# Hybrid encoder layer on one core: merged last down-projection groups, the v cast on GpSimd, and roots of norms left in PSUM

## The chip, the cores and the metric

The kernel runs on one core of a Trainium2 chip. The metric is the device time of one execution in microseconds; the time of the kernel before is the median of three runs. A profile of one execution on the chip goes with it.

## The reference

One layer of a streaming encoder, for a prompt of 2048 frames and a sample of 32 frames that continues a stream with 2048 cached frames. Everything is fp32, d_model is 1024.

```python
h = x + rmsnorm(mixer(rmsnorm(x, g_mix_pre)), g_mix_post)
y = h + rmsnorm(conv_ffn(rmsnorm(h, g_ffn_pre)), g_ffn_post)

def mixer(h):                     # one projection for both groups
    q, k, v, z, xbc, dt_raw = split(h @ w_in)        # 512 each for q, k, v, z; 768; 8
    attn = stick_breaking(q, k_all, v_all)           # 8 heads x 64, strictly causal
    xh, B, C = split(silu(causal_dwconv(xbc, 4 taps)))
    y = ssd_scan(xh, softplus(dt_raw + dt_bias), -exp(a_log), B, C) + d_skip * xh
    y = rmsnorm(y * silu(z), g_ssm_out)              # the gated norm
    return concat(rmsnorm(attn, g_attn_out), y) @ w_out

def conv_ffn(h):                  # D_FF = 2816
    gate, up = split(h @ w_up)
    return (gelu(causal_dwconv(gate, 3 taps)) * up) @ w_down
```

Results are y, the k and v rows, the SSD states and the convolution tails. `rmsnorm` divides by the root of the mean square plus 1e-6.

## The kernel before

Activations lie with channels on partitions and tokens on columns. The tokens are cut into four blocks (0 to 3) of 512, 512, 512 and 544 columns; the last holds the 32 sample frames. Each matrix product is made of three: weights and activations are split into a high part, rounded to fp32r, and the low rest, and high x high, high x low and low x high are summed in PSUM (`dense`, L123). `weight` (L95) loads a raw weight, casts its high part on ScalarE (L107), subtracts on GpSimd (L108) and keeps the result in device memory under a key; later blocks load the kept parts with one DMA (L103). Weights rotate through two buffers `w` in phase one and three afterwards.

Phase one (`phase_in`) goes block by block: the convolution channels (`wbx`, conv on VectorE at L336 and L340, sigmoid on ScalarE at L344), the v projection with tokens on partitions (two halves of 260 columns for each 128 tokens; ScalarE copies them out of two PSUM buffers at L371 or L373, casts the high part `vs` at L383, GpSimd subtracts at L384, and DMAs store both), the SSD scan, the next block's norm (`prep`, scaling at L262), k and q, the gate (`gate`, L580) and the gated norm (`gate_norm`). The gated norm takes the squares' sum over partitions with a ones-matmul of 512 columns, a ScalarE square root and a VectorE reciprocal (`rstd`, L140 to L146) and scales at L602; ScalarE and GpSimd then split into `khi` and `klo` (L606, L608). The other norms use `rstd_steps`: the sum is taken with tokens on partitions (matmuls of one column, L165), VectorE adds epsilon, GpSimd raises to the power -1/2 (L183), and a matmul with the identity spreads the root over the partitions again (L194). With `stay` the root is read from PSUM, else ScalarE copies it out (L200).

Then attention of the next block and the output and FFN work of the last one (`Tail.stream`) are woven together by `fill`; block 3's tail runs alone from about 2430 us. The FFN goes by units of 128 channels: `up` makes a unit (22 in all), `down` multiplies a group of units (GROUPS: six of three, then two of two) with `w_down` and adds to eight output tiles f0 to f7. In the last block the last two groups run for each half of the columns (272) apart; `finish` then takes the root of that half (with `of`, the epsilon of the earlier norm in it, L178 to L185), scales (L1096), adds the residual and stores.

The order on each engine comes from the tile framework's scheduler, which places instructions by a simulated time line; queues are then served in order. SP issues all DMAs.

## Time and profile before

| | us |
|---|---|
| median of three runs | 2948.01 (2941.73 to 2950.02) |
| the profiled execution, its span | 2949.99, 2948.2 |
| TensorE busy | 2815.8 (96%) |
| VectorE busy | 1712.5 (58%) |
| ScalarE busy | 1261.2 (43%) |
| GpSimd busy | 1261.3 (43%) |

In the rows, PE is TensorE, PEld its weight loads, DVE is VectorE, ACT ScalarE, POOL GpSimd, SP the engine that issues DMAs (SPq its queue). Busy time of TensorE is modelled at its ends. `PEclk` is the clock that TensorE was granted: 1.00 is 2.4 GHz, 0.50 is 1.2. A name such as `w` or `rn_v` is a tile of the program; `a<-b` writes a from b. Behind a row, `[2.54 <-ACT v L373]` says that the engine was idle for 2.54 us before it and what ended that.

### The profile page before, as it was taken

To read this page: it belongs to the slowest core of one execution; us is meant where nothing else is said; L and a number is where in the kernel's file an instruction comes from. 1 tells how busy PE (TensorE), PEld (TensorE's weight loads), DVE (VectorE), ACT (ScalarE), POOL (GpSimd) and SP (SyncE) were. 2 spreads that over 40 slices of the span, in tenths; PEclk is the share of its full clock that TensorE was granted. 3 is DMA by queue.
4 is the path that set the end of the run, shared out by engine and by line. 5 is a ranking of instruction groups with operands and counts; after the bars stand their busy time and mean duration, and the time that the engine had idled before them with its cause. 6 is when DMAs were issued, how large, how long until landed. Compare 5 with 4: busy or idle time off the path is not lost.

```text
span 2948.2 us, 44882 instructions
## 1 busy us (share of the span) xinstructions
PE 2815.8 (96%) x16687; PEld 2425.0 (82%) x16687; DVE 1712.5 (58%) x2668; ACT 1261.2 (43%) x2552; POOL 1261.3 (43%) x1061
## 2 busy tenths in 40 slices
PE   8999999989889999999999999999999999999996
PEld 6777778877778888887788888978888879999996
DVE  7666576557774555537744456786666653533334
ACT  5344444337765444436433334654444433311111
POOL 4555555435766655547322223553323224411113
PEclk9999999989999999999999999999999999999998
DMA  5646454648677777777555556656544455755555
GB/s 179 183 154 175 146 169 128 170 141 266 235 260 250 271 249 276 266 255 243 197 185 182 175 178 221 236 182 215 175 167 166 167 192 180 240 177 174 176 177 174
DMA packets 251308, 586.36 MB, mean 199 GB/s; under 512 B 66155, under 2 KB 107763, under 8 KB 222547
## 3 DMA queue, kind: packets, MB, share of 16 engines
q1 hardware_dynamic: 251090, 583.49, 59.7%
q8 instruction: 133, 2.18, 0.3%
q14 instruction: 85, 0.69, 0.1%
HBM read 445.70 MB, written 137.69 MB: 198 GB/s over the span
## 4 chain that ended last, share of the span: by engine, by line
PE 74%; DVE 14%; DMA 6%; ACT 2%; issue 2%; POOL 1%; SPq 1%; DVEq 0%; POOLq 0%; ACTq 0%
PE o L123 36%; PE u L123 12%; PE t L123 10%; PE z L815 4%; PE pa L856 4%; PE pt L834 3%; PE o L364 2%; DVE xc L340 2%; DMA acB<-acD 1%; DMA w<-wS_out 1%; DVE prow L666 1%; DVE acB L440 1%; DVE x L262 1%; DVE xc L336 1%; DVE xlo L272 1%
## 5 line engine op out<-in xcount | busy, mean ns | idle before, releaser
L123 PE MATMUL o<-xhi,w 128*128 128x512 f32 (+2 forms) x3968 | 1044.4, 345 | 31.9 <-ACT xhi L286 7.9
L123 PEld LDWEIGHTS o<-xhi,w 128*128 128x128 f32 x3968 | 697.3, 192 | 125.4 <-issue 8.1
L123 PE MATMUL o<-xlo,w 128*128 128x512 f32 (+2 forms) x1984 | 683.4, 344 | 6.4 <-DVE xlo L272 3.6
L108 POOL TENSOR_TENSOR w<-wraw,w 128x1024 fp32r<-128x1024 f32 (+2 forms) x156 | 366.8, 2352 | 237.2 <-ACT w L107 212.3
L671 POOL TENSOR_TENSOR beta<-beta,prow 128x512 f32<-128x512 f32 (+3 forms) x256 | 253.8, 993 | 439.6 <-DVE prow L666 354.0
L123 PEld LDWEIGHTS o<-xlo,w 128*128 128x128 f32 x1984 | 380.0, 192 | 51.3 <-DVE xlo L272 5.3
L123 PE MATMUL o<-ah,w 128*128 128x512 f32 x992 | 344.6, 405 | 5.3 <-DVE f L1075 4.6
L123 PE MATMUL u<-xhi,w 128*128 128x512 f32 x1056 | 349.2, 398 | 0.0
L1029 POOL TENSOR_TENSOR y<-y,gb 128x512 f32<-128x512 f32 (+1 forms) x88 | 115.8, 1317 | 534.8 <-ACT gb L1028 534.8
L839 DVE TENSOR_TENSOR wt<-pt,wt 128x512 fp32r<-128x512 f32 (+2 forms) x320 | 191.5, 602 | 153.2 <-ACT wt L838 150.5
L666 DVE TENSOR_TENSOR_SCAN prow<-gam,prow,z 128x513 f32<-128x513 f32 x192 | 245.1, 1277 | 58.9 <-ACT beta L664 56.4
L838 ACT CAST wt<-pt 128x512 fp32r<-128x512 f32 (+2 forms) x320 | 166.9, 526 | 208.6 <-PE pt L834 206.4
L123 PEld LDWEIGHTS u<-xhi,w 128*128 128x128 f32 x1056 | 198.9, 188 | 46.8
L123 PEld LDWEIGHTS o<-ah,w 128*128 128x128 f32 x992 | 188.2, 190 | 47.6 <-DVE f L1075 5.7
L663 ACT ACTIVATE gam<-z 128x512 f32<-128x512 f32 (+2 forms) x320 | 173.0, 541 | 98.8 <-PE z L815 67.4
L123 PE MATMUL u<-xlo,w 128*128 128x512 f32 x528 | 209.3, 396 | 0.0
L1021 DVE SCALAR_TENSOR_TENSOR y<-gb,cv,y 128x512 f32<-128x512 f32 (+1 forms) x176 | 163.2, 928 | 72.9 <-ACT y L1019 69.9
L107 ACT CAST w<-wraw 128x1024 fp32r<-128x1024 f32 (+2 forms) x156 | 155.2, 995 | 99.3 <-PE o L123 80.8
L123 PE MATMUL o<-al,w 128*128 128x512 f32 x496 | 197.7, 399 | 0.0
L834 PE MATMUL pt<-ident,beta 128*128 128x128 f32 x1088 | 181.1, 278 | 9.6 <-DVE rn_v L175 4.4
L123 PE MATMUL t<-xhi,w 128*128 128x272 f32 x960 | 188.9, 292 | 1.0 <-DMA w<-wS_out 0.7
L856 PE MATMUL pa<-wt,v 128*64 128x256 f32 (+3 forms) x1152 | 174.7, 281 | 8.6 <-ACT wt L838 5.4
(272 smaller groups left out, 5102.3 us busy)
## 6 DMA issues: line engine op xcount, KB each, us to landing
w<-wS_up SPq DMA_DIRECT2D x132, 1024.0 KB, 4.8
w<-wS_dn SPq DMA_DIRECT2D x72, 768.0 KB, 4.8
wS_up<-w SPq DMA_DIRECT2D x44, 1024.0 KB, 4.8
w<-wS_out SPq DMA_DIRECT2D x39, 1024.0 KB, 7.1
wraw<-wup SPq DMA_DIRECT2D x44, 512.0 KB, 5.8
k<-kS SPq DMA_DIRECT2D x80, 256.0 KB, 4.3
v<-vS SPq DMA_DIRECT2D x80, 256.0 KB, 4.2
wS_dn<-w SPq DMA_DIRECT2D x24, 768.0 KB, 4.4
```

What stands on the lines that cost most here:

```text
L107: nc.scalar.copy(hi[:, :n, :], raw[:, :n, :])
L108: nc.gpsimd.tensor_tensor(lo[:, :n, :], raw[:, :n, :], hi[:, :n, :].bitcast(F32), op=ALU.subtract)
L123: mm = nc.tensor.matmul(ps[:, : c1 - c0], l[:, k, :], at(r, k0 + k)[:, c0:c1], start=first and i == 0 and k == 0, stop=last and i == 2 and ...
L663: nc.scalar.activation(g[:, c0:512], z, AF.Sigmoid, scale=-0.125)
L666: nc.vector.tensor_tensor_scan(back(pr), back(g), z[:, 0:1].to_broadcast([P, n + 1]), self.kn.ones[:, 0:1] if prev is None else prev, op0= ...
L671: eng.tensor_tensor(b[:, :n], b[:, :n], pr[:, c0 + 1 : 513], op=ALU.mult)
L815: mm = nc.tensor.matmul(z[:, :n], q[:, P * b : P * b + P], k[:, :n], start=e == 0, stop=e == 1 and kc < s)
L834: mm = nc.tensor.transpose(t[:, P * j : P * j + P], w[:, P * j : P * j + P], kn.ident[:])
L838: nc.scalar.copy(hi, t)
L839: nc.vector.tensor_tensor(lo, t, hi.bitcast(F32), op=ALU.subtract)
L856: nc.tensor.matmul(av[:m, 2 * P * p + c0 : 2 * P * p + 2 * P], v[:, j, :m], wt[:, rest, j, c0:], start=kc == s and p + j + rest == 0, stop ...
L1021: nc.vector.scalar_tensor_tensor(y[:, :W], gb[:, i : i + W], kn.col(wc + i), y[:, :W], op0=ALU.mult, op1=ALU.add)
```

## The change

Four edits. First, in the last block the groups (18, 2) and (20, 2) become one group (18, 4): `down` is called once for each half, with weights of both kept groups loaded into one buffer by two DMAs. Second, the cast of v's high part goes from ScalarE to GpSimd. Third, the root of `prep` stays in PSUM for blocks of 512 columns, and the gated norm of blocks 0 to 2 takes its root by `rstd_narrow`, with `stay`; `rstd` is gone. Fourth, the FFN's post-norm root: GpSimd now multiplies the earlier norm's value by epsilon, once, and keeps it as `rcol`, and `finish` adds it in one VectorE step where it had four around the power.

```diff
@@ weight @@
-        if key in self.kept:
-            nc.sync.dma_start(w[:, :, :n, :].bitcast(F32), self.kept[key][:])
+        keys = key if isinstance(key, list) else [key]
+        if keys[0] in self.kept:
+            m = n // len(keys)
+            for i, k in enumerate(keys):
+                nc.sync.dma_start(w[:, :, m * i : m * i + m, :].bitcast(F32), self.kept[k][:])
             return hi, lo
@@ rstd: removed; rstd_steps @@
-        v = pool.tile([P, 8], F32, name="rn_v") if rcol is None else rcol
+        v = pool.tile([P, 8], F32, name="rn_v")
...
+                nc.vector.scalar_tensor_tensor(
+                    v[rows, cols], ps[rows, cols], 1.0 / width, of[rows, cols], op0=ALU.mult, op1=ALU.add
                 )
-            nc.vector.tensor_tensor(v[:, :nb], v[:, :nb], of[:, :nb], op=ALU.mult)
-            nc.vector.tensor_scalar(v[:, :nb], v[:, :nb], EPS, 0.0, op0=ALU.add, op1=ALU.add)
-        nc.gpsimd.tensor_tensor(v[:, :nb], v[:, :nb], self.mhalf[:, :nb], op=ALU.pow)
-        if of is not None:
-            nc.vector.tensor_tensor(v[:, :nb], v[:, :nb], of[:, :nb], op=ALU.mult)
+        w = v
+        if rcol is not None:
+            w = pool.tile([P, 8], F32, name="rn_w")
+        nc.gpsimd.tensor_tensor(w[:, :nb], v[:, :nb], self.mhalf[:, :nb], op=ALU.pow)
+        if rcol is not None:
+            nc.gpsimd.tensor_scalar(rcol[:, :nb], v[:, :nb], EPS, 0.0, op0=ALU.mult, op1=ALU.add)
+        v = w
@@ phase_in @@
-        r = kn.rstd_narrow(rp, psm, "st", [sq], nt, D)
+        r = kn.rstd_narrow(rp, psm, "st", [sq], nt, D, stay=nt <= 512)
...
-            nc.scalar.copy(vs[:, 0, :], v[:, :512])
+            nc.gpsimd.tensor_copy(vs[:, 0, :], v[:, :512])
...
-        for _ in gate_norm(kn, s, xc, tm, lambda *r: kn.rstd(rp, psm, *r, tag="rstd2")):
+        for _ in gate_norm(kn, s, xc, tm, lambda sq, *r: kn.rstd_narrow(rp, psm, "st", [sq], *r, stay=True)):
@@ Tail @@
     GROUPS = [(3 * i, 3) for i in range(6)] + [(18, 2), (20, 2)]
+    LAST = GROUPS[:6] + [(18, 4)]
...
-        j0, n = self.GROUPS[g]
+        j0, n = (self.LAST if s == NSB - 1 else self.GROUPS)[g]
...
-                kn.wp, kn.a["wdn"][c // 2][:, 2 * j0 : 2 * j0 + 2 * n, :], 2 * n, key=("dn", g, c)
+                kn.wp, kn.a["wdn"][c // 2][:, 2 * j0 : 2 * j0 + 2 * n, :], 2 * n, key=[("dn", 6, c), ("dn", 7, c)] if n == 4 else ("dn", g, c)
...
-                if j == j0 and g and g < len(groups) - 1:
+                if j == j0 and g and (g < len(groups) - 1 or s == NSB - 1):
...
-                for e in range(2):
+                for e in range(1 if s == NSB - 1 else 0, 2):
                     yield from self.down(s, g - 1 + e, acts[g - 1 + e], t, e == 1)
```

The scheduler's order moves with it. Three places follow, with the number of a row in its engine's order at its start; the number behind a name tells the buffers apart.

At the end of the program, on SP, before: `w` are the weight buffers, `wS_dn_6_0` the kept weights of group 6 for output tiles 0 and 1, `o_fconv` a result that is read from unit 21's buffer `gb`.

```order
1266 L103 DMA w_28349<-wS_dn_6_0_12138 128x2x512
1267 L103 DMA w_28367<-wS_dn_6_2_12161 128x2x512
1268 L1015 DMA o_fconv<-gb_28224 128x2
1269 L1016 DMA o_fconv<-gb_28224 128x2
1270 L103 DMA w_28385<-wS_dn_6_4_13285 128x2x512
1271 L103 DMA w_28403<-wS_dn_6_6_13308 128x2x512
1272 L103 DMA w_28422<-wS_dn_7_0_13359 128x2x512
1273 L103 DMA w_28444<-wS_dn_7_2_13390 128x2x512
```

The same place now:

```order
1271 L106 DMA w_28376<-wS_dn_6_0_12164 128x2x512
1272 L106 DMA w_28376<-wS_dn_7_0_13391 128x2x512
1273 L106 DMA w_28411<-wS_dn_6_2_12187 128x2x512
1274 L106 DMA w_28411<-wS_dn_7_2_13422 128x2x512
1275 L1008 DMA o_fconv<-gb_28250 128x2
1276 L1009 DMA o_fconv<-gb_28250 128x2
1277 L106 DMA w_28448<-wS_dn_6_4_13317 128x2x512
1278 L106 DMA w_28448<-wS_dn_7_4_13481 128x2x512
```

Each buffer is filled by two DMAs, and the two stores of `gb` stand behind four loads, not two. On VectorE, in the second half of the same place, before (`t` is an output tile in PSUM, `f_24951` to `f_24958` are the tiles f0 to f7; the scalings at L1096 and additions at L1100 belong to the first half):

```order
2180 L1096 SCALAR_TENSOR_TENSOR f_24958<-f_24958,cv,rstd 128x272
2181 L1075 TENSOR_TENSOR f_24951<-t,f_24951 128x272
2182 L1100 TENSOR_TENSOR f_24952<-f_24952,xr 128x272
2183 L1075 TENSOR_TENSOR f_24952<-t,f_24952 128x272
2184 L1075 TENSOR_TENSOR f_24953<-t,f_24953 128x272
2185 L1100 TENSOR_TENSOR f_24954<-f_24954,xr 128x272
```

And now (`f_24977` to `f_24984` are f0 to f7):

```order
2138 L1068 TENSOR_TENSOR f_24981<-t,f_24981 128x272
2139 L161 MEMSET rn_v 128x8
2140 L1089 SCALAR_TENSOR_TENSOR f_24977<-f_24977,cv,rstd 128x272
...
2147 L1089 SCALAR_TENSOR_TENSOR f_24984<-f_24984,cv,rstd 128x272
2148 L1068 TENSOR_TENSOR f_24982<-t,f_24982 128x272
2149 L1093 TENSOR_TENSOR f_24978<-f_24978,xr 128x272
2150 L1093 TENSOR_TENSOR f_24980<-f_24980,xr 128x272
2151 L1068 TENSOR_TENSOR f_24983<-t,f_24983 128x272
```

The eight scalings stood ahead of the second half's first output tile and now stand behind its fifth. In the v stretch of block 1, on ScalarE, before (`v<-o` is a copy of half a v tile, `t<-xc` a sigmoid behind the convolution):

```order
141 L373 COPY v_1883<-o_1833 128x260
142 L373 COPY v_1883<-o_1834 128x260
143 L383 CAST vs_1888<-v_1883 128x512
144 L344 ACT_TABLE_LOAD
145 L344 ACTIVATE t_1638<-xc_1601 128x512
146 L344 ACTIVATE t_1676<-xc_1601 128x512
147 L373 COPY v_1943<-o_1893 128x260
148 L373 COPY v_1943<-o_1894 128x260
```

And now:

```order
134 L365 COPY v_1889<-o_1839 128x260
135 L365 COPY v_1889<-o_1840 128x260
136 L365 COPY v_1949<-o_1899 128x260
137 L365 COPY v_1949<-o_1900 128x260
138 L365 COPY v_2009<-o_1959 128x260
139 L336 ACTIVATE t_1644<-xc_1607 128x512
140 L336 ACTIVATE t_1682<-xc_1607 128x512
141 L365 COPY v_2009<-o_1960 128x260
```

Five copies stand ahead of the first sigmoid where two did, and the cast and a table load are gone. At the end of block 0, on GpSimd, before (`w<-wraw` is a weight's low part, `klo` the low part of the gated norm's output):

```order
60 L108 TENSOR_TENSOR w_1717<-wraw_1718,w_1717 128x1024
61 L108 TENSOR_TENSOR w_1755<-wraw_1756,w_1755 128x1024
62 L608 TENSOR_TENSOR klo_1543<-xc_236,khi_1541 128x512
63 L608 TENSOR_TENSOR klo_1550<-xc_236,khi_1548 128x512
64 L108 TENSOR_TENSOR w_1793<-wraw_1794,w_1793 128x1024
65 L608 TENSOR_TENSOR klo_1557<-xc_236,khi_1555 128x512
66 L608 TENSOR_TENSOR klo_1564<-xc_236,khi_1562 128x512
```

And now (`rn_v` is the gated norm's root):

```order
64 L111 TENSOR_TENSOR w_1723<-wraw_1724,w_1723 128x1024
65 L174 TENSOR_TENSOR rn_v_1538<-rn_v_1538,mhalf_76 128x4
66 L111 TENSOR_TENSOR w_1761<-wraw_1762,w_1761 128x1024
67 L111 TENSOR_TENSOR w_1799<-wraw_1800,w_1799 128x1024
68 L600 TENSOR_TENSOR klo_1549<-xc_236,khi_1547 128x512
69 L600 TENSOR_TENSOR klo_1556<-xc_236,khi_1554 128x512
70 L111 TENSOR_TENSOR w_2408<-wraw_2409,w_2408 128x1024
71 L600 TENSOR_TENSOR klo_1563<-xc_236,khi_1561 128x512
```

The root's power stands between weights, and the low parts come behind one weight more (`w_1799` is the weight that was `w_1793`).

## Rows read from the trace of the kernel before

**Rows 1.** The page: busy us, share of span, instructions; TensorE.

```profile
PE 2815.8 (96%) x16687; PEld 2425.0 (82%) x16687; DVE 1712.5 (58%) x2668; ACT 1261.2 (43%) x2552; POOL 1261.3 (43%) x1061
```

**Rows 2.** Stretches: length, busy by engine (instructions), granted clock, DMA share, GB/s.

```profile
0.00:640.00 640.00, 588.70 (x3479) 493.71 (x3480) 424.16 (x710) 277.81 (x442) 323.79 (x198) 0.97 0.53 159
...
2892.00:2949.00 57.00, 32.26 (x220) 30.06 (x218) 29.70 (x71) 8.80 (x20) 23.19 (x26) 0.82 0.62 188
```

**Rows 3.** TensorE's waits: waiter, releaser; us in total, times, longest.

```profile
PE o L364 <- ACT v L373: 7.5, 3, 2.9
PE u L194 <- DVE rn_v L185: 6.3, 3, 3.5
...
PE t L123 <- DMA w<-wS_dn: 5.7, 7, 1.2
```

**Rows 4.** The chain that ended last: start, us, what; in the last block.

```profile
2868.30 6.03 PE t L123 x48
```

**Rows 5.** TensorE's time line in the tail: start, us, instruction [idle before].

```profile
2896.46 0.36 PE L123 MATMUL t<-ah,w 128*128 128x272 f32 x1 [1.05 <-DMA w<-wS_dn]
...
2924.25 0.39 PE L123 MATMUL t<-ah,w 128*128 128x272 f32 x1 [2.05 <-DVE f L1075]
```

**Rows 6.** Time line of all engines from 2930 us to the end.

```profile
2930.00 0.44 DVE L1075 TENSOR_TENSOR f<-t,f 128x272 f32<-128x272 f32 x1 [0.31 <-PE t L123]
...
2932.30 1.16 PE L165 MATMUL u<-ones,fsq 128*128 128x1 f32 x6 [2.34 <-POOL fsq L776]
...
2934.25 0.86 POOL L183 TENSOR_TENSOR rn_v<-rn_v,mhalf 128x3 f32<-128x3 f32 x1 [2.00 <-DVE rn_v L182]
...
2935.45 1.43 PE L194 MATMUL u<-ident,rn_v 128*128 128x128 f32 x6 [2.00 <-DVE rn_v L185]
...
2937.34 4.89 DVE L1096 SCALAR_TENSOR_TENSOR f<-f,cv,rstd 128x272 f32<-128x272 f32 x8 [2.03 <-ACT rstd L200]
```

**Rows 7.** DMA issues, 2890 to 2935 us: count, KB each, us to landing.

```profile
w<-wS_dn SPq DMA_DIRECT2D x14, 512.0 KB, 4.7
```

**Rows 8.** Time line of all engines, 2885 to 2900 us: unit 21.

```profile
2890.66 0.66 ACT L1026 ACTIVATE gb<-y 128x546 f32<-128x546 f32 x1 [2.87 <-DMA o_fconv<-gb]
...
2895.96 1.34 POOL L1044 TENSOR_TENSOR al<-y,ah 128x544 fp32r<-128x544 f32 x1 [1.72 <-ACT ah L1043]
```

**Rows 9.** TensorE's time line in phase one, two of its waits.

```profile
220.40 0.39 PE L364 MATMUL o<-wvhi,xhi 128*128 128x260 f32 x1 [2.54 <-ACT v L373]
...
314.89 0.77 PE L123 MATMUL o<-xhi,w 128*128 128x512 f32 x1 [2.86 <-DVE t L580]
```

**Rows 10.** ScalarE's time line in the v stretch of block 1.

```profile
218.79 1.29 ACT L344 ACTIVATE t<-xc 128x512 f32<-128x512 f32 x2 [4.28 <-DVE xc L340]
```

**Rows 11.** The v split by line: ns min/median/max, first and last start, forms.

```profile
L383 ACT CAST vs<-v x16: 602/620/627, 62.1 to 556.4; 128x512 fp32r<-128x512 f32 x16
...
L384 POOL TENSOR_TENSOR vs<-v,vs x16: 1283/1292/3138, 62.8 to 557.1; 128x512 fp32r<-128x512 f32 x16
```

**Rows 12.** Stretches behind those two waits of TensorE; the granted clock is third last.

```profile
221.80:225.20 3.40, 3.40 (x18) 3.40 (x17) 3.40 (x7) 2.07 (x4) 1.20 (x1) 0.50 0.22 66
...
314.00:320.70 6.70, 5.81 (x14) 4.59 (x15) 3.52 (x5) 0.63 (x1) 2.37 (x1) 0.50 0.41 146
```

**Rows 13.** Two scalings by line: root in SBUF (L262), in PSUM (L762).

```profile
L262 DVE SCALAR_TENSOR_TENSOR x<-x,cv,rstd x24: 736/748/2922, 152.7 to 480.6; 128x512 f32<-128x512 f32 x16, 128x544 f32<-128x544 f32 x8
...
L762 DVE SCALAR_TENSOR_TENSOR att<-att,cv,u x32: 467/475/500, 775.0 to 2444.5; 128x256 f32<-128x256 f32 x24, 128x272 f32<-128x272 f32 x8
```

**Rows 14.** VectorE's time line: the scalings of x for blocks 1 and 2.

```profile
152.68 9.70 DVE L262 SCALAR_TENSOR_TENSOR x<-x,cv,rstd 128x512 f32<-128x512 f32 x8
...
306.61 7.53 DVE L262 SCALAR_TENSOR_TENSOR x<-x,cv,rstd 128x512 f32<-128x512 f32 x8 [0.45 <-ACT rstd L200]
```

**Rows 15.** GpSimd's time line there.

```profile
158.85 2.98 POOL L108 TENSOR_TENSOR w<-wraw,w 128x1024 fp32r<-128x1024 f32 x1 [2.49 <-ACT w L107]
```

**Rows 16.** VectorE's time line at the gated norm of block 0.

```profile
189.63 3.35 DVE L146 RECIPROCAL rstd<-rstd 128x512 f32<-128x512 f32 x1 [11.43 <-ACT rstd L143]
```

More of the change, by code (lines that the diff above doesn't have):

```diff
@@ L133, in dense @@
             self.mark(mm)
-    def rstd(self, pool, psp, sq, n, width, tag="rstd", pt="st"):
-        nc = self.nc
-        r = pool.tile([P, 544], F32, name=tag)
-        for c0, c1 in tiles_of(n):
-            ps = psp.tile([P, 512], F32, name=pt)
-            nc.tensor.matmul(
-                ps[:, : c1 - c0], self.ones[:], sq[:, c0:c1], start=True, stop=True
-            )
-            nc.scalar.activation(
-                r[:, c0:c1], ps[:, : c1 - c0], AF.Sqrt, bias=self.eps[:], scale=1.0 / width
-            )
-        nc.vector.reciprocal(r[:, :n], r[:, :n])
-        return r
     def rstd_narrow(self, *args, **kw):
@@ L168, in rstd_steps @@
                 )
-        v = pool.tile([P, 8], F32, name="rn_v") if rcol is None else rcol
+        v = pool.tile([P, 8], F32, name="rn_v")
         if e:
             nc.vector.memset(v[:], 1.0)
-        if of is None:
-            if e:
-                nc.vector.tensor_scalar(v[:e, nf:nb], ps[:e, nf:nb], 1.0 / width, EPS, op0=ALU.mult, op1=ALU.add)
-            nc.vector.tensor_scalar(v[:, :nf], ps[:, :nf], 1.0 / width, EPS, op0=ALU.mult, op1=ALU.add)
-        else:
-            for rows, cols in ((slice(0, P), slice(0, nf)),) + (((slice(0, e), slice(nf, nb)),) if e else ()):
+        for rows, cols in ((slice(0, P), slice(0, nf)),) + (((slice(0, e), slice(nf, nb)),) if e else ()):
+            if of is None:
+                nc.vector.tensor_scalar(
+                    v[rows, cols], ps[rows, cols], 1.0 / width, EPS, op0=ALU.mult, op1=ALU.add
+                )
+            else:
                 nc.vector.scalar_tensor_tensor(
-                    v[rows, cols], ps[rows, cols], 1.0 / width, of[rows, cols], op0=ALU.mult, op1=ALU.mult
+                    v[rows, cols], ps[rows, cols], 1.0 / width, of[rows, cols], op0=ALU.mult, op1=ALU.add
                 )
-            nc.vector.tensor_tensor(v[:, :nb], v[:, :nb], of[:, :nb], op=ALU.mult)
-            nc.vector.tensor_scalar(v[:, :nb], v[:, :nb], EPS, 0.0, op0=ALU.add, op1=ALU.add)
-        nc.gpsimd.tensor_tensor(v[:, :nb], v[:, :nb], self.mhalf[:, :nb], op=ALU.pow)
-        if of is not None:
-            nc.vector.tensor_tensor(v[:, :nb], v[:, :nb], of[:, :nb], op=ALU.mult)
+        w = v
[5 more added lines that the diff above has]
+        v = w
         yield
@@ L1124, in stream @@
             done = (i for h in (0, SBS[s - 1][1] // 2) for i in self.finish(s - 1, h, h + 256, self.f))
-        groups = self.GROUPS
+        groups = self.LAST if s == NSB - 1 else self.GROUPS
         tiles = tiles_of(nt)
```

## The prediction

> **What bounds the kernel now.** I read the page first, then the table of stages, then TensorE's waits, and only then single stretches. TensorE is busy for 2815.8 us of 2948.2 [rows 1], so only idle TensorE time and TensorE time at the lower of its two clock levels can be won. By stage [rows 2], TensorE is idle for 51 us of phase one (0 to 640 us) and for 25 of the 57 from 2892 us on; in the attention and the FFN between them it is 97% full, and the change touches little there. Of the waits [rows 3] three are met by edits: ScalarE's v copies 7.5 us, the last multiply of the finish's root (L185) 6.3, and the last down-projection weights 5.7. The profiled execution took 2949.99 us (span 2948.2 and 1.8 around it); the sum is made against that, and it lies 2.0 above the median of the runs, 2948.01.
>
> **1. Merged last groups: the tail.** Two groups of two units become one of four. In the last block the matmuls stay 192: 48 take 6.03 us [rows 4], so 0.1256 each and 24.1 in all. They begin one load's work (24 matmuls, 3.0 us) before the wait of 1.05 us that ends at 2896.46 [rows 5], at 2892.4, and end at 2930.0, when VectorE starts on the last output tile [rows 6]: 37.6 us. Of the 13.5 lost, at most 2.6 are the small matmuls of the first half's finish (1.16 and 1.43 for such a pair in the end, at the low clock [rows 6]; I take 1.6), the rest are waits: for weights, like that one, and 2.05 at 2924.25 for an output tile that VectorE was late to empty [rows 5]. A 512 KB load lands 4.7 us after its issue [rows 7], is used up in 12 matmuls, 1.5 us, and there are three buffers: 4.7 + 1.5 over 3 is 2.1 us for each 1.5 of work. After, a buffer holds 1 MB for 24 matmuls, 3.0 us; the second 512 KB lands some 1.7 us after the first (an estimate: the three buffers pass one in 2.1 us, and their queue is not full), so 4.7 + 1.7 + 3.0 over 3 is 3.1 against 3.0. The weight waits are nearly gone; I leave 1 us.
>
> A new wait comes in its place. Before, the first eight output tiles used units 18 and 19 alone. Now each needs unit 21, whose low part (al) is written at 2895.96 and takes 1.34 [rows 8]: ready at 2897.3. In SP's queue one more load stands right ahead of the two output DMAs for which ScalarE waited 2.87 us [rows 8]; the whole chain behind (square, VectorE, sigmoid, GpSimd, VectorE, cast) moves by about 0.5, so 2897.8. TensorE can do ten matmuls, 1.3 us, and then stands from 2893.6 to 2897.8. The other 182 end at 2897.8 + 22.9 + 1.6 + 1.0 = 2923.3, not 2930.0: 6.7 us earlier.
>
> VectorE eats a part. In its new order the eight scalings of the first half (4.89 us a set [rows 6]) stand ahead of output tiles 5, 6 and 7 of the second. The scalings can start when the broadcast in tile 5 is copied, at about 2919.2, and end at 2924.1; three additions from PSUM at 0.44 and three others about as long lead to 2926.8 for tile 7, against 2930.4. Squares come 1.5 us apart rather than 0.75 and no longer queue at GpSimd: 3.9 gained at the ones-matmul of 2932.30. Behind it the root has one VectorE step for three before GpSimd's power, and none between the power's end at 2935.11 and the broadcast at 2935.45: 0.7 in all. Sum 4.6. The stand of 4.2 us may cost a stretch of lower clock afterwards (as below, up to 1.7), most of it inside waits that are left. **Taken: -4.0**; bounds 0 (every microsecond of the first wait lost) and -7.5.
>
> **2. The other roots.** L181, L182 and L185 go for six finishes of earlier blocks; the price of each is the same 0.7. TensorE waited there twice more, 6.3 less 2.0 [rows 3, 6] = 4.3 us. **Taken: -1.0**; bounds 0 and -2.2. The extra GpSimd multiply of the FFN roots (eight, at most the 0.86 of the power each [rows 6]) is read only a block later; if GpSimd were late there, its 7 us would show.
>
> **3. Phase one, in four pieces.**
> (a) V stretch of block 1. TensorE waited 2.54 us at 220.40 [rows 9], as the v copy stood in ScalarE's queue behind two sigmoids which waited 4.28 us for VectorE's convolution [rows 10]. The change takes the cast (0.62 [rows 11]) out, and the new order puts five v copies ahead of the first sigmoid. Blocks 0, 2 and 3 keep copies behind sigmoids. After the wait the clock was granted at 0.50 from 221.8 to 225.2 [rows 12], the 1.2 GHz level: 1.7 us of work lost. Of 4.2 in all I take -2.5.
> (b) Roots in PSUM. The scalings of x took 0.75 us in the median, but up to 2.92; the scaling of the attention output, with its root in PSUM, never exceeds 0.50 (475 ns for half the columns) [rows 13]. The eight of block 1 took 9.70 us and those of block 2 7.53 [rows 14]: three long ones, one of which fills the end of a weight's subtraction on GpSimd, 158.85 to 161.83 [rows 15]. The Trainium skill, "SBUF — State Buffer" (Who interferes with whom), says that a VectorE instruction with two SBUF inputs contends with a GpSimd one that reads SBUF, and one with a single SBUF input does not; the two lines agree. Blocks 1 and 2 (not 3, whose root goes to SBUF as before) so win 3 x 2.15 = 6.5 us of VectorE, and the copy of the root on ScalarE goes from each chain. Behind them stand the gate's products: 2.86 us idle at 314.89 [rows 9], then 6.7 us at 0.50 [rows 12]. I take -3.0 of 6.2.
> (c) The gate norm's root. 3.35 us of reciprocal go, but VectorE had been idle for 11.43 us before it [rows 16], so that gains nothing by itself. In TensorE's new order the broadcast stands some 25 matmuls of 512 columns behind the ones-matmul (25 x 0.1256 x 512/272 = 5.9 us), so the root comes no earlier, and at the end of block 0 GpSimd's low parts (klo) come one weight later, 24 matmuls or 5.7 us; the next convolution, whose tile they free, starts up to 5 us later. What covers it is that the SSD of block 1 also waits for the last v copy, at the end of the stretch. +1.5; bounds -2 and +5.
> (d) The cast on GpSimd: the trace has no such cast; ScalarE's 0.62 and GpSimd's two-input subtraction of 1.29 [rows 11] bound it. 16 of them are 10 to 21 us on an engine busy for half of phase one, beside VectorE's convolutions, which have two SBUF inputs. The nearest row is the subtraction, on the same engine, so I count about 1 us each. VectorE loses what a long scaling loses, at most a cast's length, 4 x 1.29 = 5.2 us a stretch; a third of its time is free, so +1.0; bounds 0 and +15 (three stretches, as in the last rival). The Trainium skill, in the section named above, speaks against this edit: whichever of the two engines comes second waits for the whole of the other's instruction.
> **Taken: -3.0**; bounds -11 and +10. The schedule is rebuilt between 600 and 800 us as well (the sample's scores move by some rows); I take 0 there, with 3 either way.
>
> Sum: 2949.99 - 4.0 - 1.0 - 3.0 = **2942 us**, 6 below the median: inside 0.3% (8.8 us, about what a measurement of this kernel can tell from no change; 2939.2 to 2956.8).
>
> **Rivals.**
> *Phase one opens up.* The waits of (a) and (b) go whole with their clock: 4.2 + 6.2 + 1 = 11.4, with the tail at 4.6 and 1 for the roots: 2933. For it: the long scalings end with a GpSimd instruction, and both waits stand right behind VectorE. Against: (c) gives some back.
> *Nothing moves.* The wait for unit 21 eats the weight waits: if the second load of a buffer lands 3 us rather than 1.7 after the first, the six later loads cost some 1 us each, and the low clock after the stand the rest. Roots that come 25 matmuls later are no earlier, so that half of the change does not do what it says. 2947 to 2950, say 2948.
> *Slower: GpSimd holds the convolution.* The casts delay VectorE in the stretches of blocks 0, 2 and 3, where v copies still stand behind sigmoids, by 4 x 1.29 each: 15.5, less 5 of tail and roots: 2960. It decides once the sigmoids come more than a V tile (2.9 us) later than now. For it: TensorE's waits of 2.87 at 381.70 and 2.09 at 542.30 are of this kind already, the rest of the 7.5 [rows 3]. Against: VectorE is idle a third of phase one [rows 2].
>
> **How the numbers follow.** Forecast 0.45 (2938 to 2946), phase one opens 0.25, nothing moves 0.20, slower 0.10. Faster by over 0.3%: nearly all of the second and a quarter of the first, 0.35. Slower: most of the last, 0.10. Within: 0.55. The range is 2931 to 2955: down to the second case with 2 to spare, up to half of the slower one; about 0.15 is left out.
>
> **What would show it.** Tail: one TensorE wait of 4 to 5 us near the end of the up-projection with GpSimd's al as releaser, hardly any for weights afterwards, and tiles 5 to 7 emptied after the eight scalings. Roots: no x scaling over 1 us in blocks 1 and 2. V stretches: block 1 without a wait for v copies, blocks 2 and 3 with one. Wrong: weight waits still of 5 us in the tail, a cast of 2 us, or convolutions that stand behind casts and push v copies in every block.

## The result, and the profile after

The changed kernel is slower. Its median is 2963.28 us (six runs, 2958.18 to 2967.91) against 2947.69 for the kernel before; the ratio is 1.0046, with a 95% interval of 1.0028 to 1.0064. The medians differ by 15.6 us, and the interval stands for 8 to 19 us more, where 6 less were forecast; the time lies outside the stated range. The profiled execution took 2967.91 us, its span is 2966.1, 17.9 more than before. In the changed kernel most line numbers are about eight lower than before (the v cast is L375, its subtraction L376, the convolution L328 and L332, the first product with `da` L400), while `dense` is L126.

Work has not grown. This is the line that answers to [rows 1]:

```profile
PE 2818.6 (95%) x16729; PEld 2430.9 (82%) x16729; DVE 1672.2 (56%) x2628; ACT 1240.0 (42%) x2525; POOL 1283.8 (43%) x1088
```

TensorE is busy 2.8 us longer, VectorE 40 us less, ScalarE 21 less, GpSimd 22 more. So about 15 of the 17.9 us are TensorE's idle time. Where it lies is read from four stretches that begin and end with the same instructions: up to the first score of the attention, from there to a wait of 4.37 us that both kernels have, from there to a matmul of the last up-projection that stands behind a wait in both (2.74 us for `y` on VectorE before, 5.32 for its weight now), and the rest. First the kernel before (columns as in [rows 2]):

```profile
0.00:643.80 643.80, 592.50 (x3509) 497.51 (x3510) 424.16 (x710) 278.20 (x443) 324.33 (x198) 0.97 0.53 159
643.80:771.10 127.30, 112.07 (x814) 87.41 (x813) 94.24 (x155) 91.27 (x220) 68.97 (x69) 0.95 0.77 244
771.10:2559.00 1787.90, 1745.98 (x9510) 1477.04 (x9510) 1053.47 (x1488) 819.54 (x1745) 794.41 (x731) 0.99 0.63 215
2559.00:2948.20 389.20, 365.21 (x2856) 363.02 (x2856) 140.59 (x317) 72.19 (x145) 73.64 (x63) 0.97 0.54 179
```

and the changed kernel:

```profile
0.00:657.40 657.40, 596.31 (x3552) 500.45 (x3552) 404.91 (x709) 257.34 (x416) 341.18 (x210) 0.96 0.53 155
657.40:792.00 134.60, 116.24 (x814) 93.05 (x813) 94.13 (x156) 90.90 (x220) 69.58 (x76) 0.90 0.73 231
792.00:2582.20 1790.20, 1742.08 (x9511) 1474.82 (x9511) 1042.90 (x1473) 820.82 (x1746) 801.19 (x740) 0.99 0.63 214
2582.20:2966.10 383.90, 363.92 (x2856) 362.57 (x2856) 130.29 (x292) 70.97 (x143) 71.88 (x62) 0.97 0.54 181
```

The differences are +13.6, +7.3, +2.3 and -5.3. The tail gained a little more than was forecast for it; phase one and the 130 us behind it lost four times as much. In the second stretch the clock column falls from 0.95 to 0.90 with the same 814 matmuls.

TensorE's waits (as in [rows 3]) name the place. The waits for the v copies of blocks 1 to 3 fell from 7.5 to 5.6 us (that of block 0 grew from 1.5 to 3.3) and the wait for the last down weights is gone from the list, but a wait that before was too short for it now stands at its head:

```profile
PE st L400 <- DVE da L398: 12.6, 2, 9.3
...
PE u L186 <- POOL rn_v L174: 6.7, 3, 4.1
...
PE o L356 <- ACT v L365: 5.6, 3, 2.6
PE u L155 <- POOL fsq L768: 5.5, 1, 5.5
```

`da` is the last of the small softplus steps on VectorE behind the v projection; the SSD scan of a block begins with it. The long wait is that of block 1. GpSimd's time line there, in the changed kernel:

```profile
215.62 5.18 POOL L375 CAST vs<-v 128x512 fp32r<-128x512 f32 x1 [2.04 <-ACT v L365]
220.89 6.38 POOL L376 TENSOR_TENSOR vs<-v,vs 128x512 fp32r<-128x512 f32 x1
230.07 0.91 POOL L375 CAST vs<-v 128x512 fp32r<-128x512 f32 x1 [2.79 <-DMA vS<-vs]
231.06 2.37 POOL L376 TENSOR_TENSOR vs<-v,vs 128x512 fp32r<-128x512 f32 x1
236.26 0.61 POOL L375 CAST vs<-v 128x512 fp32r<-128x512 f32 x1 [2.83 <-DMA vS<-vs]
...
238.23 2.66 POOL L251 TENSOR_TENSOR sq<-sq,t 128x512 f32<-128x512 f32 x2
```

A cast that takes 0.61 us when VectorE is quiet took 5.18, and the subtraction behind it 6.38 where 1.29 is its median [rows 11]. Beside them VectorE ran two unbroken series of convolution steps, each step at its usual 0.74 us, and then, 26 us after the first series began, the eight softplus steps (five of them shown):

```profile
215.62 4.71 DVE L332 SCALAR_TENSOR_TENSOR xc<-raw,cv,xc 128x512 f32<-128x512 f32 x7
...
220.75 5.38 DVE L332 SCALAR_TENSOR_TENSOR xc<-raw,cv,xc 128x512 f32<-128x512 f32 x8
...
241.75 1.21 DVE L389 TENSOR_SCALAR ab<-e 128x32 f32<-128x32 f32 x1 [4.30 <-ACT e L388]
243.00 1.19 DVE L391 TENSOR_SCALAR dt<-ab 128x32 f32<-128x32 f32 x1
244.22 1.20 DVE L392 TENSOR_TENSOR e<-e,dt 128x32 f32<-128x32 f32 x1
...
246.80 2.26 DVE L395 TENSOR_TENSOR lw<-lw,e 128x32 f32<-128x32 f32 x1
...
250.31 1.18 DVE L398 TENSOR_TENSOR da<-dt,nega 128x32 f32<-128x32 f32 x1
```

These have 32 columns and take some 0.2 us alone (the reciprocal 0.34); here all but the reciprocal end with the GpSimd instruction beside them, and the eight sum to 9.61 us (3.65 before). They also begin late. ScalarE's queue shows why: the exponential stands behind a square that waits for GpSimd, whose sums of squares had been pushed behind the casts. Then TensorE's row:

```profile
239.55 0.63 ACT L250 ACTIVATE t<-x 128x512 f32<-128x512 f32 x1 [2.93 <-POOL sq L251]
...
241.49 0.23 ACT L388 ACTIVATE e<-ab 128x32 f32<-128x32 f32 x1
```

```profile
251.64 0.60 PE L400 MATMUL st<-da,triu 128*128 128x32 f32 x2 [9.28 <-DVE da L398]
```

From the end of the last v copy to TensorE's first product with `da` 15.0 us passed in the changed kernel, and 8.4 before, where `da` was ready after 6.9:

```profile
241.36 0.19 DVE L406 TENSOR_TENSOR da<-dt,nega 128x32 f32<-128x32 f32 x1
```

The wait is not all that phase one lost. Of its 13.6 us 3.0 lie ahead of the first v matmul of block 1, 5.5 from there to `da`, 8.6 from there to the first v matmul of block 3, and 3.6 were won back behind it. The third of these pieces is busy time at a lower clock, not waiting: the clock fell to its lower level within the wait of 9.28 us, and over the piece the mean granted was 0.95 where it was 0.98. The 31 matmuls more are those of the narrow root; E2 (below) does as many there in 263.7 us of busy time. Before and now:

```profile
243.10:526.60 283.50, 264.54 (x1501) 216.36 (x1500) 192.36 (x305) 125.51 (x197) 155.92 (x86) 0.98 0.52 156
```

```profile
251.60:543.80 292.20, 274.73 (x1532) 225.55 (x1533) 178.61 (x304) 114.72 (x186) 160.35 (x91) 0.95 0.50 149
```

The scalings of x did become short, as [rows 13] had let one expect: in blocks 1 and 2 none is over 748 ns, while block 3, whose root still goes through SBUF, keeps a long one.

```profile
L254 DVE SCALAR_TENSOR_TENSOR x<-x,cv,st x16: 739/742/748, 155.5 to 321.8; 128x512 f32<-128x512 f32 x16
L254 DVE SCALAR_TENSOR_TENSOR x<-x,cv,rstd x8: 770/774/2940, 491.1 to 499.3; 128x544 f32<-128x544 f32 x8
```

In the tail, the wait for unit 21 is there but shorter than forecast, 1.38 and 0.77 us; no wait for weights over 1 us follows; and before the last root TensorE waits 5.47 us, since the eight scalings stand ahead of the additions of the last three tiles on VectorE:

```profile
2920.60 0.64 PE L126 MATMUL t<-ah,w 128*128 128x272 f32 x3 [1.38 <-ACT ah L1036]
2922.01 0.39 PE L126 MATMUL t<-al,w 128*128 128x272 f32 x1 [0.77 <-POOL al L1037]
...
2951.25 1.15 PE L155 MATMUL u<-ones,fsq 128*128 128x1 f32 x6 [5.47 <-POOL fsq L768]
```

```profile
2942.26 4.98 DVE L1089 SCALAR_TENSOR_TENSOR f<-f,cv,rstd 128x272 f32<-128x272 f32 x8 [0.25 <-ACT rstd L192]
2947.17 0.43 DVE L1068 TENSOR_TENSOR f<-t,f 128x272 f32<-128x272 f32 x1
```

### The profile page after: what moved, and what is told of

It reads as the page before. It is cut to its first block, busy times and chain, and to the rows that moved or that the text cites. A ratio compares the mean times of both kernels' runs of the same rounds, so it can differ in the third digit from the quotient of the medians.

```text
span 2966.1 us, 44895 instructions
## 1 busy us (share of the span) xinstructions
PE 2818.6 (95%) x16729; PEld 2430.9 (82%) x16729; DVE 1672.2 (56%) x2628; ACT 1240.0 (42%) x2525; POOL 1283.8 (43%) x1088
## 4 chain that ended last, share of the span: by engine, by line
PE 75%; DVE 12%; DMA 6%; ACT 2%; issue 2%; POOL 2%; SPq 1%; DVEq 0%; POOLq 0%; ACTq 0%
PE o L126 38%; PE u L126 12%; PE t L126 10%; PE z L807 4%; PE pa L848 4%; PE pt L826 3%; DVE prow L658 2%; DVE xc L332 1%; PE o L356 1%; DMA acB<-acD 1%; DMA w<-wS_out 1%; DVE xlo L264 1%; DMA xr<-hS 1%; DVE xc L328 1%; DVE xlo L968 1%
## 5 line engine op out<-in xcount | busy, mean ns | idle before, releaser
L126 PE MATMUL o<-xhi,w 128*128 128x512 f32 (+2 forms) x3968 | 1051.4, 347 | 27.9 <-ACT xhi L278 8.3
L126 PEld LDWEIGHTS o<-xhi,w 128*128 128x128 f32 x3968 | 702.2, 193 | 120.3 <-ACT xhi L278 8.3
L126 PE MATMUL o<-xlo,w 128*128 128x512 f32 (+2 forms) x1984 | 687.7, 347 | 7.3 <-DVE xlo L264 4.6
L126 PEld LDWEIGHTS o<-xlo,w 128*128 128x128 f32 x1984 | 382.2, 193 | 53.4 <-DVE xlo L264 7.1
L126 PE MATMUL u<-xhi,w 128*128 128x512 f32 x1056 | 349.5, 398 | 0.0
L126 PE MATMUL o<-ah,w 128*128 128x512 f32 x992 | 342.1, 402 | 4.1 <-DVE f L1068 3.0
L126 PEld LDWEIGHTS u<-xhi,w 128*128 128x128 f32 x1056 | 199.1, 189 | 46.7
L126 PEld LDWEIGHTS o<-ah,w 128*128 128x128 f32 x992 | 187.1, 189 | 46.6 <-DVE f L1068 4.4
L126 PE MATMUL u<-xlo,w 128*128 128x512 f32 x528 | 209.4, 397 | 0.0
L126 PE MATMUL o<-al,w 128*128 128x512 f32 x496 | 196.7, 397 | 0.0
L126 PE MATMUL t<-xhi,w 128*128 128x272 f32 x960 | 188.9, 292 | 3.2 <-DMA w<-wS_out 2.5
```

What stands on the lines that cost most here:

```text
L126: mm = nc.tensor.matmul(ps[:, : c1 - c0], l[:, k, :], at(r, k0 + k)[:, c0:c1], start=first and i == 0 and k == 0, stop=last and i == 2 and ...
```

## The experiments

The theory at the start: the cast on GpSimd falls beside VectorE's convolutions and holds both engines. The rivals: the narrow root of the gated norm delays the block; or only the two edits together do harm. "Narrow" is the root taken with tokens on partitions. Ratios are to the kernel before, measured again beside each group of experiments (medians from 2948.2 to 2950.0).

**E1, the cast alone.**

```diff
-            nc.scalar.copy(vs[:, 0, :], v[:, :512])
+            nc.gpsimd.tensor_copy(vs[:, 0, :], v[:, :512])
```

> The kernel before with one edit: the cast of vs is issued on GpSimd instead of ScalarE. Theory (the cast holds GpSimd and VectorE: in the changed kernel one cast took 5.18 us and the subtraction behind it 6.38 us beside VectorE's convolution, and the squares and the softplus of the block come later): slower than before by 6 to 14 us, about 2957, with L400-type waits of TensorE (for da) of several us in block 1. Rival (the gated norm's narrow root is what delays the block): 2946 to 2950, no wait for da. Second rival (only the two edits together, which put five v copies ahead of the first sigmoid, make the wait): within 4 us of before, casts over 2 us but no wait for da.

Measured: 2950.06 us, ratio 1.0003 (0.9991 to 1.0016). The theory falls: alone, the cast costs nothing that can be measured. Its longest took 1.14 us, and there is no long wait for `da`. The second rival stands, though its casts of over 2 us did not come.

**E2, all of the change but the cast.**

```diff
-            nc.gpsimd.tensor_copy(vs[:, 0, :], v[:, :512])
+            nc.scalar.copy(vs[:, 0, :], v[:, :512])
```

> The changed kernel with one edit undone: the cast of vs is back on ScalarE. Theory: phase one loses the 9.28 us wait for da in block 1 and most of the 3.30 in block 2; the time falls by 8 to 16 us from the changed kernel, to 2947 to 2955. Rival (narrow gated norm): it stays within 4 us of the changed kernel, 2959 to 2966. Second rival (the two together): as the theory, since either one undone is enough.

Measured: 2941.82, ratio 0.9971 (0.9957 to 0.9984): 21.5 below the changed kernel, more than any of the three had said. GpSimd's row in block 1 and TensorE's wait for `da` are these:

```profile
209.99 5.21 POOL L376 TENSOR_TENSOR vs<-v,vs 128x512 fp32r<-128x512 f32 x1 [2.70 <-ACT vs L375]
218.65 3.04 POOL L376 TENSOR_TENSOR vs<-v,vs 128x512 fp32r<-128x512 f32 x1 [3.45 <-ACT vs L375]
```

```profile
237.83 0.38 PE L400 MATMUL st<-da,triu 128*128 128x32 f32 x2 [2.96 <-DVE da L398]
```

The subtraction waits for the same convolutions here, 5.21 us, but once: the 5.18 of the cast ahead of it are ScalarE's 0.62.

**E3, the merged last groups alone.**

```diff
+    LAST = GROUPS[:6] + [(18, 4)]
...
-        j0, n = self.GROUPS[g]
+        j0, n = (self.LAST if s == NSB - 1 else self.GROUPS)[g]
...
-                kn.wp, kn.a["wdn"][c // 2][:, 2 * j0 : 2 * j0 + 2 * n, :], 2 * n, key=("dn", g, c)
+                kn.wp, kn.a["wdn"][c // 2][:, 2 * j0 : 2 * j0 + 2 * n, :], 2 * n, key=[("dn", 6, c), ("dn", 7, c)] if n == 4 else ("dn", g, c)
...
-                for e in range(2):
+                for e in range(1 if s == NSB - 1 else 0, 2):
```

> The kernel before with the last block's last two groups merged into one of four units, nothing else. Theory: the tail is shorter by 4 to 5 us, as the end of the changed kernel shows against before (388.2 us from the start of the last up-projection's second stage before, 383.1 after): 2943 to 2945. Rival (the gain of the tail comes from the shorter root, or is eaten by the wait for unit 21): 2946 to 2950.

Measured: 2945.87, ratio 0.9993 (0.9979 to 1.0007). The median is 3.8 lower, between the two ranges, and the interval holds no change. In its profile the last of the four stretches takes 385.6 us against 389.2: -3.6, near the -4.0 of the forecast. Up to the first score, where it does the work of before in the same order, its profile is 3.2 us shorter, which tells how far single profiles can be trusted.

**E4, the roots of phase one alone.**

```diff
-        r = kn.rstd_narrow(rp, psm, "st", [sq], nt, D)
+        r = kn.rstd_narrow(rp, psm, "st", [sq], nt, D, stay=nt <= 512)
...
-        for _ in gate_norm(kn, s, xc, tm, lambda *r: kn.rstd(rp, psm, *r, tag="rstd2")):
+        for _ in gate_norm(kn, s, xc, tm, lambda sq, *r: kn.rstd_narrow(rp, psm, "st", [sq], *r, stay=True)):
```

> The kernel before with the roots alone changed: prep's root stays in PSUM for blocks of 512 and the gated norm of blocks 0 to 2 is taken with tokens on partitions. Theory (the cast is to blame): 2941 to 2950, since the v stretch of block 1 loses its waits of 2.5 us while the root of the gated norm comes no earlier. Rival (narrow gated norm delays the block): 2954 to 2962, phase one longer by 8 us or more. Second rival (the two edits together): within 4 us of before.

Measured: 2945.42, ratio 0.9983 (0.9972 to 0.9994). Not slower, so the first rival falls too. The first score comes at 630.2 us, 13.6 earlier than before, and half of that is gone by the wait of 4.37 us, which comes 7.3 earlier.

**E5, the changed kernel with the gated norm's root as before** (`rstd`, L140, is put back).

```diff
-        for _ in gate_norm(kn, s, xc, tm, lambda sq, *r: kn.rstd_narrow(rp, psm, "st", [sq], *r, stay=True)):
+        for _ in gate_norm(kn, s, xc, tm, lambda *r: kn.rstd(rp, psm, *r, tag="rstd2")):
```

> The changed kernel with the gated norm's root as before (ones-matmul of 512 columns, square root, reciprocal); the cast stays on GpSimd, prep's root in PSUM, the groups merged. Theory (the narrow gated norm lets five v copies go ahead of the first sigmoid, so that the first cast and its subtraction fall beside VectorE's convolutions): the order goes back, two casts of 5 us at most 1.5 us each, the wait for da under 3 us, 2944 to 2952. Rival (prep's root in PSUM is what does not go with the cast): 2958 to 2966.

Measured: 2937.82, ratio 0.9952 (0.9934 to 0.9970), below even the theory's range. Two v copies instead of five go ahead of the first sigmoid of block 1, and the casts there, two of them beside convolutions still, are short:

```profile
214.31 1.05 POOL L389 CAST vs<-v 128x512 fp32r<-128x512 f32 x1 [1.96 <-ACT v L379]
215.44 1.61 POOL L390 TENSOR_TENSOR vs<-v,vs 128x512 fp32r<-128x512 f32 x1
222.78 1.14 POOL L389 CAST vs<-v 128x512 fp32r<-128x512 f32 x1 [5.72 <-ACT v L379]
```

The first of them stood in a series of seven steps without a gap, as in the changed kernel, and yet it went in between two of them; VectorE's next two steps waited for it and its subtraction:

```profile
214.81 1.09 DVE L346 SCALAR_TENSOR_TENSOR xc<-raw,cv,xc 128x512 f32<-128x512 f32 x1
215.83 1.77 DVE L346 SCALAR_TENSOR_TENSOR xc<-raw,cv,xc 128x512 f32<-128x512 f32 x1
```

So it is not enough that a cast meets a series of steps: in the changed kernel GpSimd is kept waiting until the series ends. That goes with the narrow root, whichever engine casts: in the seven kernels that have it one of GpSimd's instructions on `vs` in block 1 takes 5.2 to 6.4 us, in the seven others none takes more than 3.2. What in the new order of VectorE's steps does it was not tested.

**E6, prep's root back in SBUF.**

```diff
-        r = kn.rstd_narrow(rp, psm, "st", [sq], nt, D, stay=nt <= 512)
+        r = kn.rstd_narrow(rp, psm, "st", [sq], nt, D)
```

> The changed kernel with prep's root copied to SBUF as before; the narrow gated norm, the cast on GpSimd and the merged groups stay. Theory (narrow gated norm and cast together): no better than the changed kernel, 2958 to 2968. Rival (prep's root in PSUM and the cast together): 2944 to 2952.

Measured: 2961.38, ratio 1.0041 (1.0025 to 1.0056). Prep's root has no part in the loss: the first cast of block 1 takes 5.18 us again, and TensorE waits 9.32 for `da`.

**E7, the cast back on ScalarE in block 1 alone.**

```diff
-            nc.gpsimd.tensor_copy(vs[:, 0, :], v[:, :512])
+            (nc.scalar.copy if s == 1 else nc.gpsimd.tensor_copy)(vs[:, 0, :], v[:, :512])
```

> The changed kernel with the cast on ScalarE in block 1 alone, on GpSimd in blocks 0, 2 and 3. Theory (the cost is the place beside the convolution, worst in block 1, where the first cast and subtraction took 11.6 us and TensorE waited 9.28 for da): 9 to 14 us less than the changed kernel, 2949 to 2954, and the wait for da in block 1 about 3 us as in the kernel with all casts on ScalarE. Rival (the casts cost the same in every block, 21 us over four): 4 to 6 less, 2957 to 2959.

Measured: 2945.52, ratio 0.9988 (0.9978 to 0.9999): 17.8 less than the changed kernel, from four casts. The place in block 1 is the cause, as the theory had it by then, and the rival of equal costs falls. The wait for `da` is 3.12 us. The size is beyond the 9 to 14 expected. In the profiles 7.4 us of it lie ahead of block 1's `da` and 12.6 from there to the first v matmul of block 3, where the changed kernel waited 3.30 us for block 2's `da` too and was granted 0.95, not 0.98, for the same work:

```profile
245.30:524.90 279.60, 267.45 (x1531) 220.12 (x1532) 185.67 (x304) 116.38 (x189) 167.11 (x94) 0.98 0.53 159
```

**E8, two buffers for `vs`.**

```diff
-            vs = sd.tile([P, 2, 512], F32R, name="vs", bufs=1)
+            vs = sd.tile([P, 2, 512], F32R, name="vs", bufs=2)
```

> The changed kernel with two buffers for vs instead of one, so that a cast on GpSimd need not wait until the store of the one before has landed (21.7 us of GpSimd's idle time in seven waits, with squares and splits queued behind). Theory (shared time with VectorE's convolution costs, not the wait): the first casts stay long, 2956 to 2966. Rival (the store's wait at the head of GpSimd's queue costs): the waits go, the squares come earlier, 2945 to 2953.

Measured: 2946.55, ratio 0.9996 (0.9984 to 1.0008), the rival's time. The rival's reason is seen, but is not enough: GpSimd's waits for the stores are gone (21.7 us in the changed kernel), and `da` of block 1 comes 3.0 us sooner after the first v matmul. Yet the casts beside the convolutions are as long as the theory had said, and TensorE still waits 6.33 us for `da`.

```profile
213.36 5.18 POOL L375 CAST vs<-v 128x512 fp32r<-128x512 f32 x1 [2.04 <-ACT v L365]
218.63 6.38 POOL L376 TENSOR_TENSOR vs<-v,vs 128x512 fp32r<-128x512 f32 x1
224.95 3.76 POOL L375 CAST vs<-v 128x512 fp32r<-128x512 f32 x1
```

Hence four more kernels, to complete the table of cast, gated norm and buffers.

**E9, cast on ScalarE and the gated norm as before** (E5's and E2's edits together).

```diff
-            nc.gpsimd.tensor_copy(vs[:, 0, :], v[:, :512])
+            nc.scalar.copy(vs[:, 0, :], v[:, :512])
...
-        for _ in gate_norm(kn, s, xc, tm, lambda sq, *r: kn.rstd_narrow(rp, psm, "st", [sq], *r, stay=True)):
+        for _ in gate_norm(kn, s, xc, tm, lambda *r: kn.rstd(rp, psm, *r, tag="rstd2")):
```

> The changed kernel with both the cast back on ScalarE and the gated norm's root as before: of the change only the merged groups, prep's root in PSUM and the shorter roots are left. It closes the square of cast (ScalarE, GpSimd) by gated norm (before's, narrow), whose other three corners are the changed kernel 2963, cast on ScalarE 2942, gated norm as before 2938. Theory (cast and narrow gated norm cost only together): 2940 to 2946, the tail 4 to 5 us shorter than before, the time from the first v matmul to da in block 1 within 1 us of 36.8. Rival (the cast on GpSimd is a gain by itself with the gated norm as before): 2945 to 2950, clearly above 2938.

Measured: 2936.95, ratio 0.9955 (0.9940 to 0.9971), below the theory's range. It equals E5, so with the gated norm as before the cast costs 0.9 us, which is nothing that can be measured. Of what changed in phase one only prep's root is left here, and its first score comes at 632.1 us, against 643.8 in the kernel before and 640.6 in E3.

**E10, E5 with two buffers for `vs`** (E8's edit on E5).

```diff
-            vs = sd.tile([P, 2, 512], F32R, name="vs", bufs=1)
+            vs = sd.tile([P, 2, 512], F32R, name="vs", bufs=2)
```

> The kernel with the cast on GpSimd, the gated norm as before and the merged groups, with two buffers for vs. Theory (the store's wait at the head of GpSimd's queue holds the scan of block 0, whose four state products took 49.8 us with one buffer and 46.7 before): block 0's scan falls by 3 to 4 us, the whole to 2933 to 2937. Rival (the wait is hidden elsewhere, or the schedule rebuilt behind it gives it back): 2936 to 2945.

Measured: 2941.87, ratio 0.9969 (0.9956 to 0.9981). Block 0's scan does fall, from 49.8 to 46.1 us, but the whole does not: the rival's range holds.

**E11, E2 with two buffers for `vs`** (the same edit on E2).

```diff
-            vs = sd.tile([P, 2, 512], F32R, name="vs", bufs=1)
+            vs = sd.tile([P, 2, 512], F32R, name="vs", bufs=2)
```

> The kernel with the cast on ScalarE, the narrow gated norm and the merged groups, with two buffers for vs. ScalarE waits 12.7 us for stores in six waits there, with v copies queued behind. Theory (those waits are covered, TensorE waits under 3 us for da): 2939 to 2944, as with one buffer. Rival (they hold the v copies): 2932 to 2938.

Measured: 2928.49, ratio 0.9932 (0.9914 to 0.9950), the fastest of all, some 20 us under the kernel before. The time is lower than either had said, and the rival's reason isn't what the profile shows; E2's second and third stretch, then E11's:

```profile
630.90:765.40 134.50, 114.95 (x814) 91.97 (x813) 93.73 (x156) 90.76 (x220) 69.59 (x76) 0.92 0.73 232
765.40:2556.90 1791.50, 1744.24 (x9511) 1475.98 (x9511) 1041.72 (x1473) 820.84 (x1746) 800.63 (x740) 0.98 0.63 214
```

```profile
631.20:757.40 126.20, 112.34 (x815) 87.44 (x813) 95.18 (x155) 91.09 (x220) 69.13 (x70) 0.96 0.77 246
757.40:2541.30 1783.90, 1740.03 (x9510) 1471.59 (x9511) 1042.60 (x1473) 820.08 (x1746) 802.50 (x740) 0.99 0.63 215
```

Phase one, where `vs` is used, is the same in both (630.9 and 631.2). The gain is 8.3 us behind it and 7.6 in the long stretch that follows; for the latter no cause is seen. This fastest kernel also shows that a long wait of GpSimd need not cost: in block 1 three subtractions take 5.20 us and, the next two, 10.34, which is 11.7 over their usual 1.29 each (the first cast and subtraction of the changed kernel: 9.7), and TensorE waits 3.97 us for `da`.

```profile
212.22 5.20 POOL L376 TENSOR_TENSOR vs<-v,vs 128x512 fp32r<-128x512 f32 x1 [2.71 <-ACT vs L375]
217.94 10.34 POOL L376 TENSOR_TENSOR vs<-v,vs 128x512 fp32r<-128x512 f32 x2 [0.52 <-ACT vs L375]
```

**E12, E11 with the gated norm as before** (E5's edit).

```diff
-        for _ in gate_norm(kn, s, xc, tm, lambda sq, *r: kn.rstd_narrow(rp, psm, "st", [sq], *r, stay=True)):
+        for _ in gate_norm(kn, s, xc, tm, lambda *r: kn.rstd(rp, psm, *r, tag="rstd2")):
```

> The cast on ScalarE, the gated norm's root as before, the merged groups, prep's root in PSUM, and two buffers for vs: the last kernel (cast on ScalarE, narrow gated norm, two buffers, 2928) with the gated norm as before. It tells whether the narrow root pays by itself once nothing else turns with it. Theory (the narrow root saves phase one 4 to 5 us by v copies that go ahead of the sigmoids, and cost only with the cast on GpSimd or through the order of the sample's scores): 2932 to 2937. Rival (the narrow root is worth nothing, the second buffer is the gain): 2926 to 2931.

Measured: 2939.17, ratio 0.9965 (0.9953 to 0.9976), a little above the theory's range and far above the rival's. With two buffers the narrow root is worth 10.7 us.

**The table.** Medians in us; in brackets, from one profile each: the time from the first v matmul of block 1 to its first product with `da`; the scan of block 0 from its first product with `da` to its last transpose of B (L476), just ahead of the last state products; the stretch from the first score to the wait of 4.37 us. The kernel before has 36.9, 46.7 and 127.3.

| | narrow gated norm | gated norm as before |
|---|---|---|
| cast on ScalarE, one `vs` | 2941.8 (34.9, 46.5, 134.5) | 2937.0 (37.5, 46.4, 126.4) |
| cast on GpSimd, one `vs` | 2963.3 (42.4, 50.2, 134.6) | 2937.8 (37.0, 49.8, 129.0) |
| cast on ScalarE, two `vs` | 2928.5 (35.9, 46.4, 126.2) | 2939.2 (36.2, 46.5, 129.8) |
| cast on GpSimd, two `vs` | 2946.6 (39.4, 46.0, 126.1) | 2941.9 (35.2, 46.1, 125.9) |

Moving the cast to GpSimd costs 21.5 and 18.1 us with the narrow root, 0.9 and 2.7 without it. The second buffer saves 13.3 and 16.7 with the narrow root, whichever engine casts, and nothing that stands out without it (2.2 and 4.1 us more, where the kernel before differs by up to 2.3 among the groups of runs); so E8's gain is not GpSimd's wait for the stores alone. Of the 25.0 us between E8's profile and that of the changed kernel 11.6 lie in phase one, where that wait is seen in block 0's scan (50 against 46), and 8.5 in the stretch behind it.

The third number explains a part of it. All five kernels with the narrow root and one buffer (the changed one, E2, E4, E6, E7) need 133 to 136 us there, the nine others (the kernel before among them) 126 to 131; the nearest two are 2.5 us apart. In those five, 18 matmuls of block 3's gate stand between the first score and the sample's first, in the others 2; the sample's first score then comes 11.6 to 13.2 us after the first score, not 8. In the changed kernel the first 15 us of this stretch have 56 matmuls and a granted clock of 0.66, in E8 77 and 0.77:

```profile
657.40:672.40 15.00, 12.23 (x56) 9.58 (x54) 5.71 (x12) 8.89 (x21) 9.79 (x14) 0.66 0.52 150
```

```profile
645.80:660.80 15.00, 12.62 (x77) 10.38 (x76) 8.14 (x16) 9.85 (x26) 6.85 (x7) 0.77 0.62 180
```

This order goes with the time in fourteen kernels; no kernel was run in which it alone was changed, so it is not shown to be the cause.

## Why the prediction was wrong

**The step that failed is the sum of part 3: (a) and (d) were added as if they were independent.** (a) booked -2.5 us because five v copies go ahead of the first sigmoid of block 1; (d) booked +1.0 for the casts and looked for their harm in blocks 0, 2 and 3, where copies stand behind sigmoids. It is the other way round. Each number is near the truth by itself: with the cast on ScalarE, the narrow root shortens the way from the first v matmul to `da` from 37.5 to 34.9 us (E9, E2), -2.6; without the narrow root the cast costs 0.9 (E9, E5). With the narrow root the same cast costs 21.5 (E2), 17.8 of them in block 1 (E7). The copies that come early are not the whole reason: in E5 too the first cast falls among seven convolution steps, but there it gets in between them.

**Two bounds of (d) were wrong with it.** A loss of "at most a cast's length" on VectorE named the wrong loser: in block 1 VectorE's convolution steps kept their 0.74 us, and GpSimd's cast and subtraction lost 9.7 (5.18 and 6.38 against 0.61 and 1.29). The Trainium skill, "SBUF — State Buffer" (Who interferes with whom), says that whichever instruction comes first holds the shared ports for its whole length; the traces agree for one instruction (the step beside E5's cast took 1.09 us for 0.74), and show that against a series of seven or eight steps in a row GpSimd may have to wait for the whole series. And (d) priced the cast without what is queued behind it on GpSimd: the sums of squares, behind them ScalarE's squares and the exponential, and then eight small VectorE steps, seven of which each wait for one GpSimd instruction. That chain was in the trace of before, 8.4 us with 3.65 of VectorE's, and I did not look at it, since TensorE hardly waited there. Nor did the sum hold the time at the lower clock that follows such a wait. The bounds of the four pieces of part 3 add up to -12 and +20; taking -11 and +10 left out the +13.6 that phase one came to.

**(a)'s reason** was half wrong: the new order of copies and sigmoids comes with the narrow root, with either engine (E2 and E4 have it, E1 and E5 not). The wait of 2.54 us for a v copy in block 1 is 1.15 in the changed kernel, and gone in E2.

**(b)**, -3.0 of at most 6.2, was too small where nothing hides it: in E9, with prep's root alone, phase one is 8.5 us shorter than in E3 and 11.7 shorter than before. Beside the narrow root and the cast it is not there: E6, without it, is 1.9 us below the changed kernel, within the spread of the runs. No scaling in blocks 1 and 2 is over 748 ns, as foreseen; how much of the gain is theirs is open. That an operation with one SBUF input is free of GpSimd holds for these scalings and not for every one: `tensor_scalar` took 1.21 us beside it, and 0.18 without.

**(c)**, +1.5 with bounds -2 and +5: in E2 against E9 phase one is 1.2 us shorter, in E11 against E12 3.3. Its cost lay elsewhere, in the next step.

**600 to 800 us**, taken at 0 with 3 either way, was +7.3. This was mis-sized with the order at hand: that the sample's scores move by some rows was seen, but not that 16 more gate matmuls ahead of them could cost time in a stretch where TensorE waits for VectorE's scans. That these matmuls are the cause is not shown. It was partly luck that the changed kernel with the cast on ScalarE (E2) came near the forecast, 7.9 us below the kernel before: its phase one is 12.9 shorter where the other pieces made 4.0, and the stretch behind it 7.2 longer.

**Tail**, -4.0: right, -5.3 in the changed kernel and -3.6 with the merge alone. The wait for unit 21 was 2.2 us, not 4.2: TensorE had 27 matmuls to do before it, not ten. The weight waits are gone, tiles 5 to 7 are emptied behind the scalings, and a wait of 5.47 us before the last root replaces that of 2.34 [rows 6].

**Other roots**, -1.0: the price of 0.7 is right where it can be read, in the last finish (2.00 us of waiting before, 1.31 now), but the sum is not seen in the time. In all TensorE waits 6.7 us in three places for these roots, against 7.7 in four; one wait grew from 3.49 to 4.06. The third stretch is 2.3 longer, and it ends with a wait that grew by 2.6: it is 2.7 in the four kernels without the fourth edit, and 4.9 to 5.4 in the ten with it. What in the edit does that is open.

Of the rivals, the slower one came nearest in time (2960) and in its title, GpSimd and the convolution, with the block and the loser exchanged; it had a chance of 0.10.
